# Weight sums of the output projections on VectorE, four low parts moved into the next unit, additions of the plain tiles put first

## The chip, the cores and the metric

The kernel runs on one core of one Trainium2 chip. The metric is the device time of one execution in microseconds (us); the times of a kernel are given as the median of its runs with the lowest and the highest. The core has five engines, each with an instruction queue of its own: TensorE (PE in the profile, its weight loads PEld), VectorE (DVE), ScalarE (ACT), GpSimd (POOL) and SyncE (SP), which here issues the transfers.

## The reference, cut to what matters

Two layers are run over 1024 prompt tokens and 8 sample tokens together. Layer 0 mixes tokens with a gated linear recurrence, layer 1 with a chunked spatial gate. What concerns us is the end of both mixers: an output projection from 2048 to 1024 channels, whose result is added to the residual.

```python
def hgrn2_mixer(h, s0, w_in, lb, g_norm, w_out):
    ...
    return (o * jax.nn.silu(z)) @ w_out, S          # (1032, 2048) @ (2048, 1024)

def chunk_mlp_mixer(h, w_in, ln_g, ln_b, w_sp, b_sp, w_out):
    ...
    y = (u * s * jax.nn.silu(z)) @ w_out             # (1032, 2048) @ (2048, 1024)

def trunk(...):
    ...
        h = h + y
        gate = jax.nn.sigmoid(rmsnorm(h, norm_ple[i]) @ w_ple_gate[i])
        h = h + gate * (p[i] @ w_ple_proj[i])
```

All of it is float32.

## The kernel before, in words

**Products.** Activations lie with channels on the 128 partitions and tokens along the rows. The 1032 tokens are three column blocks, c = 0, 1, 2, of 384, 384 and 264 columns (`CH`, `W`). TensorE is fed with a 32-bit format of its own, so every float32 operand is split into a high part, a cast on ScalarE, and a low part, the difference, on VectorE (`split_weights`, L150 and L151; `split`, L219 and L220; `load_list`, L372 and L376). `mm3` (L224 to L226) makes one product of three matmuls: high times high, high times low, low times high.

**Output projection.** `out_phase` runs once for each layer (keys "oa" and "ob"). The 2048 input channels are taken in two halves of 1024 (f = 0 and 1), the 1024 output channels in eight tiles m of 128. In each half the tiles m = 0 and 1 are "plain": one accumulation in a PSUM bank for each c (`plain`). The tiles 2 to 7 (in the second half 2 to 5) go in pairs through `unit`: seven products instead of eight for the blocks c = 0 and 1, as in a Strassen-Winograd step, and a plain product for c = 2 (`last`). A unit needs four sums of blocks of its weights (s1 to s4) and four sums of blocks of the operand (t1 to t4). Tiles 6 and 7 of the second half are plain again.

**Weights.** `load_unit` fetches two weight tiles of 512 KB with SyncE (L189), forms the four sums in the tile `ssum` with four operations of 512 columns (L193, L195, L198, L200), and splits both tiles and the four sums. Tile names: `wstg` and `wstg3` are staged weights, `whi` and `wlo` the parts of a weight tile, `shi` and `slo` those of a sum. Before the change the four operations run on GpSimd for all units of the kernel. The units of the projection into layer 1 (key "B") pass no f; those of the output projections pass f.

**Additions.** A finished product is added to the residual rows `h` on VectorE (`add`, L1061), directly from PSUM for plain tiles, for c = 2 and for the first of a unit's four results. The three PSUM banks of the tag "mm" (`ps_o`, `ps_proj`) are used in turn by the plain tiles and by the products of a unit: a product can start only when the addition that empties its bank has run. In the second half each addition is followed by a square on ScalarE (`sql`, L259) and its sum on VectorE (`ssq`, L260).

**Inside a unit.** The order of the products on TensorE is: a11 (bank `ps1`), s2, a12 (added onto `ps1`), the c = 2 product of the first tile, s1, s3 (bank `ps_d`), s4, a22 (added onto `ps_d`), the c = 2 product of the second tile. With `early` a c = 2 product comes first. Between a11 and a12 ScalarE copies `ps1` into `u2` (L954), and between s3 and a22 VectorE reads `ps_d` (`c22`, L977). `after(i)` calls hooks between the products.

**Operand of the second half.** While the first half is computed, `mix_second` loads blocks of the second half's operand, forms their sums (`mix_rows`, L418 to L421) and stores them; one step of it (`mix1`) is called from hooks. The last unit of the first half calls `exchange`, which lists 40 transfers for the second half's operand; each step of the list (`jobs`) casts one staged tile, subtracts for its low part (L372, L376) and fetches the tile seven places further on. Twenty steps run in hooks of that unit, twenty behind the first five of the six plain products that follow. The last four of the list belong to t4, which the a22 product of the next unit reads.

**Order.** TensorE's order is the program's. On the other engines a scheduler orders instructions when the program is built; `tc.high_priority(offset=PRI)` moves what it encloses ahead, and `issue_after` holds an instruction behind another. Each engine runs its queue in the order that results. In the profile the output projection of layer 0 lies between about 764 and 935 us, that of layer 1 between about 1614 and 1786 us.

Of the kernel before, what the change touches and what calls it, by code (L numbers as in the profile page):

```python
# [13 lines left out]
ALU = mybir.AluOpType  # L14
# [5 lines left out]
KT = D // P  # L20
# [10 lines left out]
PRI = 400  # L31
# [50 lines left out]
def trunk_kernel(ctx, tc, xT, st, pT, nrm, wina, lbl, gna, wouta, winb, lng, lnb, lngr, lnbr,  # L82
# [95 lines left out]
    def load_unit(key, m, f=None):  # L178


        a = []
        for _ in range(2):

            a.append(ws[0].tile([P, 1024], F32, name="wstg3", bufs=1) if nst[0] % 3 == 2 else
                     wp.tile([P, 1024], F32, name="wstg"))
            nst[0] += 1
        with tc.high_priority(offset=0 if f is None else PRI):
            for i in range(2):
                nc.sync.dma_start(a[i], winb[m + i] if f is None else wsrc[key.lower()][m + i, f])  # L189
        a11, a12, a21, a22 = (a[i][:, j * 512:(j + 1) * 512] for i in range(2) for j in range(2))  # L190
        w0 = split_weights(a[0], 1024, PLAIN, wp)
        t = ws[0].tile([P, 512], F32, name="ssum", bufs=2)
        G.tensor_tensor(t, a21, a22, ALU.add)  # L193
        s1 = split_weights(t, 512, SUMS, ws[0])
        G.tensor_tensor(t, t, a11, ALU.subtract)  # L195
        s2 = split_weights(t, 512, SUMS, ws[0])
        t3 = ws[0].tile([P, 512], F32, name="ssum", bufs=2)
        G.tensor_tensor(t3, a11, a21, ALU.subtract)  # L198
        s3 = split_weights(t3, 512, SUMS, ws[0])
        G.tensor_tensor(t, a12, t, ALU.subtract)  # L200
        s4 = split_weights(t, 512, SUMS, ws[0])
        w1 = split_weights(a[1], 1024, PLAIN, wp)
        return w0, w1, (s1, s2, s3, s4)
# [797 lines left out]
    def out_phase(key, b, ssq, first, done, pre, begin):  # L1001
# [3 lines left out]
        with ExitStack() as s:  # L1005
# [51 lines left out]
            seen = set()  # L1057

            def add(m, c, src, end):
                with tc.high_priority(offset=PRI if end and m >= KT - 2 else 0):  # L1060
                    V.tensor_tensor(hr[c][m], hr[c][m], src[:, :W[c]], ALU.add)  # L1061
                if end:
                    accum_sq(sp, ssq[c], hr[c][m], c not in seen, m == KT - 1, W[c], V if m < 9 else G, True)
                    seen.add(c)
                    if m == KT - 1:
                        done(c)
# [43 lines left out]
            def units(f, ms, then):  # L1110
                for m in ms:
                    wt = take(key.capitalize(), m, f)
                    ex, hooks = then.get(m, (None, {}))
                    bb = dict(b)
                    if ex:
                        ex()
                    unit(wt, bb, up, lambda i, c, src: add(m + i, c, src, f == 1),
                         early=int(f == 0 and m in (2, KT - 2)),
                         then=hooks)
# [29 lines left out]
            def last_exchange():  # L1149
# [1 line left out]
                gen[0] = load_list(quarter("b12"), zr, ZR, False)  # L1151
                steps(gen[0], ZR)()

            units(0, range(2, KT, 2), {2: (rows_of(2), {5: mix1}), 4: (rows_of(4), {1: mix1, 5: mix1, 7: mix1}),
                                       KT - 2: (exchange, {2: jobs(4), 3: jobs(4), 5: jobs(6), 7: jobs(6)})})
            for m in range(2):
                wt = take(key, m, 1)
                for c in CH:
                    ps = plain(bank(), wt, c)
                    if (m, c) != (1, 2):  # L1160
                        jobs(4)()
                    add(m, c, ps, True)
            assert next(gen[0], None) is None
            units(1, range(2, KT - 2, 2), {KT - 4: (last_exchange, {4: jobs(4)})})
            wts = [take(key, m, 1) for m in (KT - 2, KT - 1)]
            for c in CH:
                for m, wt in zip((KT - 2, KT - 1), wts):
# [468 lines left out]
```

## Time and profile before

| what | before |
|---|---|
| median of 3 runs (lowest to highest) | 1910.68 us (1909.73 to 1911.68) |
| profiled execution, its own time | 1912.36 us |
| its span, first to last instruction | 1910.6 us |
| mean granted TensorE clock | 0.988 |

The stages of the two output projections, from a table of stretches of that execution (busy us of each engine; clock as a share of full speed; DMA as mean busy share of the 16 transfer engines):

| stage | stretch | us | PE | DVE | ACT | POOL | clock | DMA |
|---|---|---|---|---|---|---|---|---|
| layer 0, plain tiles, first half | 764 to 792 | 28 | 28.00 | 17.12 | 11.95 | 5.91 | 1.00 | 0.79 |
| layer 0, three units | 792 to 854 | 62 | 60.29 | 46.98 | 20.98 | 11.06 | 1.00 | 0.81 |
| layer 0, plain tiles, second half | 854 to 880 | 26 | 22.66 | 22.51 | 17.77 | 6.05 | 0.98 | 0.67 |
| layer 0, two units and tiles 6, 7 | 880 to 935 | 55 | 55.00 | 34.13 | 18.46 | 5.97 | 0.95 | 0.29 |
| layer 1, plain tiles, first half | 1614 to 1640 | 26 | 25.38 | 15.06 | 14.60 | 4.70 | 1.00 | 0.91 |
| layer 1, three units | 1640 to 1704 | 64 | 59.97 | 44.49 | 19.83 | 11.69 | 1.00 | 0.76 |
| layer 1, plain tiles, second half | 1704 to 1731 | 27 | 24.40 | 24.16 | 17.70 | 6.07 | 1.00 | 0.70 |
| layer 1, two units and tiles 6, 7 | 1731 to 1786 | 55 | 54.09 | 34.49 | 18.62 | 6.38 | 0.94 | 0.24 |

The rest of the profile is read in the prediction. In its rows an arrow `<-` after idle time names what ended the wait; x behind a row counts instructions merged into it.

### The profile page before, as it was taken

What the parts mean: (1) busy time and instruction counts of PE and PEld (TensorE: products, weight loads), DVE (VectorE), ACT (ScalarE), POOL (GpSimd) and SP (SyncE); (2) the same over time, 40 slices, a digit from 0 to 9 for tenths busy, and PEclk for the clock granted to TensorE, in tenths of its full rate; (3) what the DMA queues carried; (4) which work ended last, traced back from release to release, by engine and by line L of the source; (5) the groups of instructions that cost most, each with busy time, mean ns of one, the idle gap of its engine ahead of it and who ended that gap; (6) DMA issues with size and microseconds to landing.
All of it is one profiled execution on the core that took longest, in us unless ns stands there. A gap on an engine that the chain in (4) does not pass through costs nothing.

```text
span 1910.6 us, 34453 instructions
## 1 busy us (share of the span) xinstructions
PE 1869.5 (98%) x13130; PEld 1840.8 (96%) x13130; DVE 1329.5 (70%) x2941; ACT 864.4 (45%) x1853; POOL 448.8 (23%) x445
## 2 busy tenths in 40 slices
PE   8999999999999999999999999999999999999997
PEld 8999999999999999999999999999999999999997
DVE  5967676767767677677664845577778876677655
ACT  6453545444444546434344544433443345344342
POOL 3110001010010001212132323245444551302221
PEclk8999999999999999999999999999999999999998
DMA  6132323333222325873333343323334536872223
GB/s 214 64 116 79 108 72 111 128 127 111 81 91 79 108 67 179 287 232 121 100 120 120 117 143 92 100 81 105 125 126 144 175 104 209 269 236 79 71 89 111
DMA packets 155479, 243.15 MB, mean 127 GB/s; under 512 B 15089, under 2 KB 130481, under 8 KB 154289
## 3 DMA queue, kind: packets, MB, share of 16 engines
q1 hardware_dynamic: 155312, 240.94, 38.5%
q8 instruction: 103, 1.69, 0.4%
q14 instruction: 64, 0.52, 0.1%
HBM read 175.49 MB, written 65.40 MB: 126 GB/s over the span
## 4 chain that ended last, share of the span: by engine, by line
PE 42%; DVE 6%; DMA 4%; issue 2%; ACT 1%; POOL 1%; SPq 0%; DVEq 0%; POOLq 0%; ACTq 0%
PE ps_proj L224 10%; PE ps_proj L226 10%; PE ps_proj L225 10%; PE ps_d L224 2%; PE ps_d L225 2%; PE ps_d L226 2%; DMA raw<-ozd 1%; PE psp L1427 1%; PE pt_g L1309 1%; PE ps_o L224 1%; PE ps_o L225 1%; PE ps_o L226 1%; DMA h<-d3t 1%; DVE bl L376 1%; DVE tmp L298 1%
## 5 line engine op out<-in xcount | busy, mean ns | idle before, releaser
L224 PE MATMUL ps_proj<-bh,whi 128*128 128x384 f32 (+1 forms) x2392 | 766.6, 320 | 9.8 <-DVE h L1061 6.1
L226 PE MATMUL ps_proj<-bh,wlo 128*128 128x384 f32 (+1 forms) x2392 | 750.9, 314 | 1.5 <-DVE wlo L151 1.5
L225 PE MATMUL ps_proj<-bl,whi 128*128 128x384 f32 (+1 forms) x2392 | 749.5, 313 | 1.5 <-POOL bl L220 1.5
L224 PEld LDWEIGHTS ps_proj<-bh,whi 128*128 128x128 f32 x2392 | 452.3, 189 | 12.2 <-issue 6.8
L225 PEld LDWEIGHTS ps_proj<-bl,whi 128*128 128x128 f32 x2392 | 452.6, 189 | 2.0 <-POOL bl L220 2.0
L226 PEld LDWEIGHTS ps_proj<-bh,wlo 128*128 128x128 f32 x2392 | 451.2, 189 | 2.7 <-DVE wlo L151 2.7
L151 DVE TENSOR_TENSOR wlo<-wstg,whi 128x1024 fp32r<-128x1024 f32 x148 | 184.8, 1249 | 100.6 <-ACT whi L150 99.6
L150 ACT CAST whi<-wstg 128x1024 fp32r<-128x1024 f32 x148 | 155.0, 1047 | 139.3 <-PE ps_proj L225 123.0
L150 ACT CAST shi<-ssum 128x512 fp32r<-128x512 f32 x128 | 79.2, 621 | 159.7 <-PE ps_proj L225 77.8
L151 DVE TENSOR_TENSOR slo<-ssum,shi 128x512 fp32r<-128x512 f32 x128 | 102.2, 800 | 15.9 <-ACT shi L150 15.5
L193 POOL TENSOR_TENSOR ssum<-wstg 128x512 f32<-128x512 f32 x32 | 48.4, 1513 | 225.6 <-DMA wstg<-in_winb 69.1
L224 PE MATMUL ps_proj<-xmh,shi 128*128 128x384 f32 x244 | 84.3, 345 | 1.1 <-DVE h L1061 0.8
L225 PE MATMUL ps_proj<-xml,shi 128*128 128x384 f32 x244 | 82.9, 340 | 1.4 <-DVE xml L220 1.4
L226 PE MATMUL ps_proj<-xmh,slo 128*128 128x384 f32 x244 | 82.8, 339 | 0.0
L220 POOL TENSOR_TENSOR ql<-q,qh 128x384 fp32r<-128x384 f32 (+1 forms) x24 | 22.2, 927 | 253.4 <-ACT qh L219 253.4
L716 DVE TENSOR_TENSOR q<-q,t 128x192 f32<-128x192 f32 (+1 forms) x144 | 47.2, 329 | 40.0 <-PE pC L713 33.6
L224 PE MATMUL ps_o<-bh,whi 128*128 128x384 f32 (+1 forms) x232 | 73.2, 315 | 0.0
L225 PE MATMUL ps_o<-bl,whi 128*128 128x384 f32 (+1 forms) x232 | 72.7, 313 | 0.0
L226 PE MATMUL ps_o<-bh,wlo 128*128 128x384 f32 (+1 forms) x232 | 72.6, 313 | 0.0
L1436 POOL TENSOR_TENSOR s<-s,u 128x384 f32<-128x384 f32 (+1 forms) x48 | 54.1, 1128 | 67.7 <-DVE s L1430 67.1
L233 POOL TENSOR_TENSOR rsq<-ss_e,mhalf 128x3 f32<-128x3 f32 (+2 forms) x32 | 24.1, 752 | 194.4 <-DVE ss_e L753 194.4
L195 POOL TENSOR_TENSOR ssum<-ssum,wstg 128x512 f32<-128x512 f32 x32 | 43.2, 1349 | 105.7 <-DVE slo L151 102.7
(339 smaller groups left out, 3958.2 us busy)
## 6 DMA issues: line engine op xcount, KB each, us to landing
wstg<-in_wina SPq DMA_DIRECT2D x48, 512.0 KB, 3.7
wstg<-in_winb SPq DMA_DIRECT2D x48, 512.0 KB, 3.7
raw<-ozd SPq DMA_DIRECT2D x48, 192.0 KB, 3.7
pj<-ppd SPq DMA_DIRECT2D x16, 516.0 KB, 5.0
S<-in_st SPq DMA_DIRECT2D x16, 512.0 KB, 4.5
vb<-vd SPq DMA_DIRECT2D x16, 512.0 KB, 4.8
out_so_s<-S SPq DMA_DIRECT2D x16, 512.0 KB, 3.5
wstg<-in_wouta SPq DMA_DIRECT2D x16, 512.0 KB, 3.9
```

Of the source, the lines that this page charges most:

```text
L150: A.copy(hi, src)
L151: V.tensor_tensor(lo, src, hi.bitcast(F32), ALU.subtract)
L193: G.tensor_tensor(t, a21, a22, ALU.add)
L195: G.tensor_tensor(t, t, a11, ALU.subtract)
L220: last["lo"] = eng.tensor_tensor(lo, src, hi.bitcast(F32), ALU.subtract)
L224: PE.matmul(ps, wh, xh, start=first, stop=False, skip_group_check=more)
L225: PE.matmul(ps, wh, xl, start=False, stop=False, skip_group_check=more)
L226: PE.matmul(ps, wl, xh, start=False, stop=last, skip_group_check=more)
L233: G.tensor_tensor(y, e, mhalf[:, :n], ALU.pow)
L298: V.scalar_tensor_tensor(t[:, :w], src(j), g32[:, gi, j:j + 1], pbc[:, :w], ALU.mult, ALU.mult)
L716: V.tensor_tensor(ql[:, :, 1, :], ql[:, :, 1, :], t2[:, :, 0:1].broadcast_to([P, n, lv]), ALU.mult)
L1436: G.tensor_tensor(s[:, :w], s[:, :w], us[mm, c][:, :w], ALU.mult)
```

## The change

It has three parts. The four weight sums of the units of the output projections (`load_unit` with an f) go from GpSimd to VectorE: five units for each layer, 40 operations in all; the units of the projection into layer 1 keep theirs on GpSimd. Of the twenty steps of the operand exchange behind the plain tiles of the second half the last four move to a hook behind the first product of the next unit. And the additions of the plain tiles m = 0 and 1 of the second half get the high priority that those of tiles 6 and 7 had. Besides, one `mix1` of the second unit of the first half is called one product later.

```diff
--- before.py
+++ after.py
@@ -190,14 +190,15 @@
         t = ws[0].tile([P, 512], F32, name="ssum", bufs=2)
-        G.tensor_tensor(t, a21, a22, ALU.add)
+        eng = G if f is None else V
+        eng.tensor_tensor(t, a21, a22, ALU.add)
         s1 = split_weights(t, 512, SUMS, ws[0])
-        G.tensor_tensor(t, t, a11, ALU.subtract)
+        eng.tensor_tensor(t, t, a11, ALU.subtract)
         s2 = split_weights(t, 512, SUMS, ws[0])
         t3 = ws[0].tile([P, 512], F32, name="ssum", bufs=2)
-        G.tensor_tensor(t3, a11, a21, ALU.subtract)
+        eng.tensor_tensor(t3, a11, a21, ALU.subtract)
         s3 = split_weights(t3, 512, SUMS, ws[0])
-        G.tensor_tensor(t, a12, t, ALU.subtract)
+        eng.tensor_tensor(t, a12, t, ALU.subtract)
@@ -1057,7 +1058,7 @@
             def add(m, c, src, end):
-                with tc.high_priority(offset=PRI if end and m >= KT - 2 else 0):
+                with tc.high_priority(offset=PRI if end and (m >= KT - 2 or m < 2) else 0):
                     V.tensor_tensor(hr[c][m], hr[c][m], src[:, :W[c]], ALU.add)
@@ -1151,17 +1152,16 @@
-            units(0, range(2, KT, 2), {2: (rows_of(2), {5: mix1}), 4: (rows_of(4), {1: mix1, 5: mix1, 7: mix1}),
+            units(0, range(2, KT, 2), {2: (rows_of(2), {5: mix1}), 4: (rows_of(4), {2: mix1, 5: mix1, 7: mix1}),
                                        KT - 2: (exchange, {2: jobs(4), 3: jobs(4), 5: jobs(6), 7: jobs(6)})})
             for m in range(2):
                 wt = take(key, m, 1)
                 for c in CH:
                     ps = plain(bank(), wt, c)
-                    if (m, c) != (1, 2):
+                    if (m, c) < (1, 1):
                         jobs(4)()
                     add(m, c, ps, True)
-            assert next(gen[0], None) is None
-            units(1, range(2, KT - 2, 2), {KT - 4: (last_exchange, {4: jobs(4)})})
+            units(1, range(2, KT - 2, 2), {2: (None, {1: jobs(5)}), KT - 4: (last_exchange, {4: jobs(4)})})
```

TensorE's order is the same in both kernels. In the changed file a line stands one lower between L193 and L1162, so the sums are L194, L196, L199 and L201 there, low parts of the exchange L377, additions to `h` L1062, sums of squares L261 and the read of `ps_d` L978.

VectorE, layer 0, second half, from the addition of tile 0 with c = 2 on (`h_0_10252`; `h_1_10237`, `h_1_10245` and `h_1_10253` are tile 1 with c = 0, 1, 2; `xml` and `bl` are low parts of the exchange), before:

```order
L1061 TENSOR_TENSOR h_0_10252<-h_0_10252,ps_o 128x264
L151 TENSOR_TENSOR wlo<-wstg,whi 128x1024
L376 TENSOR_TENSOR bl_140<-raw,bh_137 128x384
L151 TENSOR_TENSOR slo<-ssum,shi 128x512 x2
L376 TENSOR_TENSOR bl_140<-raw,bh_137 128x384 x3
L151 TENSOR_TENSOR slo<-ssum,shi 128x512
L376 TENSOR_TENSOR bl_140<-zr,bh_137 128x384
L1061 TENSOR_TENSOR h_1_10237<-h_1_10237,ps_o 128x384
L376 TENSOR_TENSOR bl_139<-zr,bh_136 128x384 x2
L260 TENSOR_TENSOR ssq_10263<-ssq_10263,sql 128x384
L376 TENSOR_TENSOR bl_139<-raw,bh_136 128x384 x2
L1061 TENSOR_TENSOR h_1_10245<-h_1_10245,ps_o 128x384
```

The same queue in the changed kernel, in two pieces; first from the two sums of the next unit's weights, which now stand in it, to the addition of tile 1 with c = 0:

```order
L194 TENSOR_TENSOR ssum<-wstg 128x512
L199 TENSOR_TENSOR ssum<-wstg 128x512
L377 TENSOR_TENSOR xml_10221<-raw,xmh_10220 128x384
L151 TENSOR_TENSOR slo<-ssum,shi 128x512
L377 TENSOR_TENSOR bl_140<-zr,bh_137 128x384
L1062 TENSOR_TENSOR h_0_10252<-h_0_10252,ps_o 128x264
L377 TENSOR_TENSOR bl_140<-zr,bh_137 128x384
L151 TENSOR_TENSOR wlo<-wstg,whi 128x1024
L377 TENSOR_TENSOR bl_140<-zr,bh_137 128x384
L377 TENSOR_TENSOR bl_140<-raw,bh_137 128x384
L196 TENSOR_TENSOR ssum<-ssum,wstg 128x512
L377 TENSOR_TENSOR bl_140<-raw,bh_137 128x384
```

The next row is the addition of tile 1 with c = 0 (L1062, `h_1_10237`), and behind it, up to the addition with c = 2:

```order
L151 TENSOR_TENSOR slo<-ssum,shi 128x512 x2
L201 TENSOR_TENSOR ssum<-wstg,ssum 128x512
L377 TENSOR_TENSOR bl_140<-raw,bh_137 128x384 x2
L151 TENSOR_TENSOR slo<-ssum,shi 128x512
L377 TENSOR_TENSOR bl_140<-zr,bh_137 128x384
L1062 TENSOR_TENSOR h_1_10245<-h_1_10245,ps_o 128x384
L261 TENSOR_TENSOR ssq_10263<-ssq_10263,sql 128x384
L377 TENSOR_TENSOR bl_139<-zr,bh_136 128x384
L194 TENSOR_TENSOR ssum<-wstg 128x512
L261 TENSOR_TENSOR ssq_10264<-ssq_10264,sql 128x384
L199 TENSOR_TENSOR ssum<-wstg_11448,wstg 128x512
L1062 TENSOR_TENSOR h_1_10253<-h_1_10253,ps_o 128x264
```

The addition of tile 1 with c = 0 moved ahead of three low parts of weights and of three of the exchange, that with c = 1 ahead of the four of t4 (`bl_139`), and six of the weights' sums now stand among them, the last two (L194, L199) those of the unit after the next.

VectorE at the start of the output projection of layer 1 (`h_0` are additions of tile 0 in the first half, whose banks the first unit needs), before:

```order
L220 TENSOR_TENSOR xml_10221<-h_6_19309,xmh_10220 128x384
L151 TENSOR_TENSOR slo<-ssum,shi 128x512
L220 TENSOR_TENSOR xml_10219<-raw,xmh_10218 128x384
L151 TENSOR_TENSOR slo<-ssum,shi 128x512
L1061 TENSOR_TENSOR h_0_19295<-h_0_19295,ps_o 128x384
```

And in the changed kernel:

```order
L221 TENSOR_TENSOR xml_10221<-h_6_19309,xmh_10220 128x384
L194 TENSOR_TENSOR ssum<-wstg 128x512
L199 TENSOR_TENSOR ssum<-wstg 128x512
L151 TENSOR_TENSOR slo<-ssum,shi 128x512
L221 TENSOR_TENSOR xml_10219<-raw,xmh_10218 128x384
L196 TENSOR_TENSOR ssum<-ssum,wstg 128x512
L1062 TENSOR_TENSOR h_0_19295<-h_0_19295,ps_o 128x384
```

Three sums came in ahead of the first addition, and the second low part of a sum moved behind it.

VectorE in the second unit of the first half, layer 0, where one `mix1` is called later (`raw` are blocks of the second half's operand; the last row reads `ps_d`), before:

```order
L419 TENSOR_TENSOR raw<-raw 128x384
L420 TENSOR_TENSOR raw<-raw 128x384
L1061 TENSOR_TENSOR h_4_10256<-h_4_10256,ps_proj 128x264
L421 TENSOR_TENSOR raw<-raw 128x384
L151 TENSOR_TENSOR wlo<-wstg,whi 128x1024
L970 TENSOR_TENSOR u_10831<-ps_proj,u_10763 128x384
L151 TENSOR_TENSOR slo<-ssum,shi 128x512
L977 TENSOR_TENSOR c_10846<-ps_d,u_10831 128x384
```

And in the changed kernel:

```order
L420 TENSOR_TENSOR raw<-raw 128x384
L1062 TENSOR_TENSOR h_4_10256<-h_4_10256,ps_proj 128x264
L421 TENSOR_TENSOR raw<-raw 128x384
L151 TENSOR_TENSOR wlo<-wstg,whi 128x1024
L971 TENSOR_TENSOR u_10831<-ps_proj,u_10747 128x384
L151 TENSOR_TENSOR slo<-ssum,shi 128x512
L422 TENSOR_TENSOR raw<-raw 128x384
L201 TENSOR_TENSOR ssum<-wstg,ssum 128x512
L978 TENSOR_TENSOR c_10846<-ps_d,u_10831 128x384
```

Between the first of these rows, which waits for a transfer of `raw`, and the read of `ps_d` there is one operation more, a sum.

## The prediction

> **What bounds the kernel now.** I read the page's busy times first, then the list of who TensorE waited for, then, at each wait, the rows of the engines in order of time.
>
> ```profile
> PE 1869.5 (98%) x13130; PEld 1840.8 (96%) x13130; DVE 1329.5 (70%) x2941; ACT 864.4 (45%) x1853; POOL 448.8 (23%) x445
> ...
> PE ps_proj L224 <- DVE h L1061: 6.8, 3, 3.3
> PE ps_d L224 <- DVE c L977: 3.2, 3, 1.6
> ...
> PE ps_proj L224 <- ACT xmh L219: 1.7, 1, 1.7
> ...
> PE ps_proj L225 <- DVE xml L220: 1.4, 1, 1.4
> ```
>
> TensorE is busy 98% of the span, so only its waits, and the slow clock behind them, can be won (columns: total us, times, longest). These four entries, 13.1 us, all lie in the two output projections, which the change touches. The largest stands where the second half's plain tiles end and the next unit begins. TensorE's rows there (start, duration), layer 0, then layer 1:
>
> ```profile
> 876.32 0.28 PE L226 MATMUL ps_o<-bh,wlo 128*128 128x264 f32 x1
> 879.95 0.66 PE L224 MATMUL ps_proj<-bh,whi 128*128 128x384 f32 x1 [3.34 <-DVE h L1061]
> 880.40 0.52 PE L225 MATMUL ps_proj<-bl,whi 128*128 128x384 f32 x1
> ...
> 885.89 0.37 PE L224 MATMUL ps_proj<-xmh,shi 128*128 128x384 f32 x1
> 886.10 0.34 PE L225 MATMUL ps_proj<-xml,shi 128*128 128x384 f32 x1
> 886.27 0.34 PE L226 MATMUL ps_proj<-xmh,slo 128*128 128x384 f32 x1
> ...
> 1728.11 0.28 PE L226 MATMUL ps_o<-bh,wlo 128*128 128x264 f32 x1
> 1731.11 0.41 PE L224 MATMUL ps_proj<-bh,whi 128*128 128x384 f32 x1 [2.71 <-DVE h L1061]
> ...
> 1739.29 0.34 PE L225 MATMUL ps_proj<-bl,whi 128*128 128x384 f32 x1
> ```
>
> At full clock starts lie 0.17 us apart (886.10 to 886.27). After the wait they lie 0.32 apart until 885.89: the clock was halved. From 876.32 to 886.10 there are 9.8 us and 20 steps, one of 264 columns (0.12) and 19 of 0.173, worth 3.4: **6.4 us are lost**. In layer 1, 1728.11 to 1739.29 is 11.2 us for 0.12 and 25 steps, 4.45: **6.7 us lost**. What VectorE did meanwhile:
>
> ```profile
> 870.04 2.58 DVE L376 TENSOR_TENSOR bl<-zr,bh 128x384 fp32r<-128x384 f32 x3
> ...
> 872.89 1.22 DVE L151 TENSOR_TENSOR wlo<-wstg,whi 128x1024 fp32r<-128x1024 f32 x1
> 874.02 0.55 DVE L376 TENSOR_TENSOR bl<-raw,bh 128x384 fp32r<-128x384 f32 x1
> 874.49 1.28 DVE L151 TENSOR_TENSOR slo<-ssum,shi 128x512 fp32r<-128x512 f32 x2
> 875.70 2.57 DVE L376 TENSOR_TENSOR bl<-raw,bh 128x384 fp32r<-128x384 f32 x3
> ...
> 879.26 0.54 DVE L1061 TENSOR_TENSOR h<-h,ps_o 128x384 f32<-128x384 f32 x1
> ```
>
> VectorE has no gap here (the rows left out fill 878.2 to 879.3). The addition that frees the bank (879.26) stands behind low parts nobody needs yet, though its product was done about 870. Before it lies a matter of order, not of work.
>
> **The change, part by part.** *Sums.* 40 operations leave GpSimd for VectorE.
>
> ```profile
> L151 DVE TENSOR_TENSOR slo<-ssum,shi x128: 672/691/1781, 777.6 to 1751.5; 128x512 fp32r<-128x512 f32 x128
> L193 POOL TENSOR_TENSOR ssum<-wstg x32: 1281/1294/2322, 775.7 to 1731.7; 128x512 f32<-128x512 f32 x32
> ...
> 848.32 1.49 DVE L376 TENSOR_TENSOR xml<-raw,xmh 128x384 fp32r<-128x384 f32 x3
> ```
>
> No such sum runs on VectorE before. The nearest row is `slo`: same size, two float32 inputs from SBUF; 0.69 alone, 0.60 a step in a row (1.28 for two). I take 0.60; GpSimd's 1.29 is the upper bound, 0.47 (a step of 384 columns, from 1.49 for three) the lower. What VectorE gets back is seen in the same rows: three low parts take 1.49 at 848.32, but 2.58 at 870.04, while GpSimd adds (its L195 ran at 870.20). About 1.1 us for each clash goes, against 0.6 for the sum, so VectorE's load hardly changes.
>
> *Additions first.* In the order rows the addition for the first bank (tile 1, c = 0) has six low parts fewer ahead of it and three sums more. From which time the new queue runs is set by the weights' transfer, since sums now wait in VectorE's own queue:
>
> ```profile
> 860.96 0.33 SPq L189 DMA_DIRECT2D wstg<-in_wouta  x1
> ...
> 866.72 1.29 POOL L193 TENSOR_TENSOR ssum<-wstg 128x512 f32<-128x512 f32 x1 [37.80 <-DMA wstg<-in_wouta]
> ...
> 885.33 0.42 ACT L259 ACTIVATE sql<-h 128x264 f32<-128x264 f32 x1
> 885.66 0.46 ACT L954 COPY u<-ps_proj 128x384 f32<-128x384 f32 x1
> ...
> 1717.87 1.29 POOL L193 TENSOR_TENSOR ssum<-wstg 128x512 f32<-128x512 f32 x1 [38.57 <-DMA wstg<-in_woutb]
> ...
> wstg<-in_wouta SPq DMA_DIRECT2D x16, 512.0 KB, 3.9
> ```
>
> From 866.7 I add the new rows: up to tile 1's c = 0 addition stand three sums (1.8), six steps of 384 columns (2.8), one `slo` (0.6), one step of 264 (0.34) and one `wlo` (1.13, from 872.89 to 874.02): 6.7 us, so it runs at 873.4. Its bank is due at 876.4: this wait goes. Up to the c = 1 addition come four more steps of 384, three `slo` and a sum, 4.3 us: 877.7, done 878.2, its bank due 12 matmuls behind the first, at 878.5. Up to the c = 2 addition come four steps and two sums, 3.1 us: 880.8; its bank is due at 882.7. But on ScalarE its square stands ahead of the copy `u2` (885.33, 885.66), without which a12 cannot begin: 0.42 for the addition, 0.35 for the square and 0.46 for the copy give 882.0, while a12 is due at 876.44 + 24 x 0.173 = 880.6. So a **new wait of 1.4 us** appears, up to 2.1 where VectorE also waits for a high part or for the next weights; I take 1.9. In layer 1 the weights land at 1717.87 and a12 is due at 1732.4: 0.8 to 1.5, I take 1.3. Gains: 6.4 - 1.9 = 4.5 and 6.7 - 1.3 = 5.4.
>
> *Four low parts moved.* Four casts, four subtractions (1.9 us of VectorE) go behind the c = 1 addition; no transfer goes with them, as the list's fetches run seven steps ahead. They are read by a22, 14 us later: cost nothing; within the sum above.
>
> *Heads of the first units.*
>
> ```profile
> 787.61 0.33 SPq L189 DMA_DIRECT2D wstg<-in_wouta  x1
> 787.98 3.29 SPq L1221 DMA_DIRECT2D h<-d0t  x7
> ...
> 798.59 0.45 PE L225 MATMUL ps_proj<-xml,shi 128*128 128x384 f32 x1 [1.40 <-DVE xml L220]
> ...
> 1637.52 1.54 POOL L195 TENSOR_TENSOR ssum<-ssum,wstg 128x512 f32<-128x512 f32 x1 [0.63 <-DVE slo L151]
> ...
> 1640.35 1.35 DVE L1061 TENSOR_TENSOR h<-h,ps_o 128x384 f32<-128x384 f32 x3
> ...
> 1641.05 0.36 PE L224 MATMUL ps_proj<-bh,whi 128*128 128x264 f32 x1 [1.66 <-ACT xmh L219]
> ```
>
> In layer 1 the bank's addition (1640.35) waits behind a `slo` for GpSimd's L195; with sums of 0.6 it ends near 1638.2, before its due time 1639.2: -1.7, less 0.2 where the next sum waits for its weights. In layer 0 seven row fetches (787.98), the last of which the waited-for `xml` reads, stand in SyncE's queue behind a weight fetch that a missing buffer holds until 787.61. Now three of the seven stand ahead of it (1.4 us of issue at 0.47 each), and the buffer comes free earlier, by four sums 0.7 shorter less two operations put ahead, about 1.8 us. Together 3.2 us against a wait of 1.4: -1.4.
>
> *Second units.*
>
> ```profile
> 1673.78 0.56 DVE L419 TENSOR_TENSOR raw<-raw 128x384 f32<-128x384 f32 x1 [3.93 <-DMA raw<-ozd]
> ...
> 1677.85 0.55 DVE L977 TENSOR_TENSOR c<-ps_d,u 128x384 f32<-128x384 f32 x1
> ```
>
> L419 waits for a transfer and `c` follows 4.1 us behind it; now L200 stands between: +0.6 in layer 1, where TensorE waits for `c`, +0.2 in layer 0, where it waited 0.2. The late `mix1` moves no transfer ahead; the stores and fetches of `raw` keep to the same releases within 1 us. I count 0 for the third wait (1.6, third units).
>
> **Sum**: -4.5 - 5.4 - 1.5 - 1.4 + 0.8 = -12.0 us. The profiled execution took 1912.36 us (1.8 around its span), 1.7 above the median; it would become 1900.4, and the median 1910.7 - 12.0 = **1898.7**.
>
> **Rivals.**
>
> *The clock halves again.* Which wait is long enough?
>
> ```profile
> 753.28 0.69 PE L759 MATMUL pt_o<-ident,on 128*128 128x128 f32 x2 [2.37 <-DVE ss_e L753]
> ...
> 754.09 0.52 PE L225 MATMUL ps_pple<-bl,whi 128*128 128x384 f32 x1
> 754.41 0.52 PE L226 MATMUL ps_pple<-bh,wlo 128*128 128x384 f32 x1
> ```
>
> 2.37 us was enough (steps of 0.32 after it), 1.66 at 1641.05 was not. My new waits of 1.9 and 1.3 lie near that. The price is what the first case shows, 18 steps at 0.32 for 0.17, 2.8 us each: 1901.5 with one, 1904.3 with both. [...]
>
> *The DMA sets the pace.* TensorE comes earlier to transfers that do not: the heads' 2.9 us are waited out later (third units), the new waits grow by 0.6 each and halve the clock: -12.0 + 2.9 + 1.2 + 5.6 = -2.3, so 1908.4. For it: L419's 3.93 idle. Against it: the stores that gate these fetches follow VectorE, which follows TensorE.
>
> *Slower: weights late in VectorE's queue.* GpSimd could wait 37.80 us for weights and hurt nobody; VectorE's sums hold up everything behind them, the banks' additions too. The transfer took 5.8 us (860.96 to 866.72). If it lands x later, the new waits are 1.9 + x and 1.3 + x, with halved clock 2.8 each: 1898.7 + 5.6 + 2x. Slower by 0.2% needs x above 5.1; at 6 it is 1916.3. For it: transfers are dense there; against: such a fetch lands after 3.9 us in the median. [...]
>
> That the change does not do what it says is excluded by the order rows.
>
> **How the numbers follow.** Forecast 0.62, clock 0.20, DMA pace 0.11, slower 0.07. If all new waits and the third units' 1.6 vanished, 1898.7 - 3.2 - 1.6 = 1893.9: the low end, 1894. The high end, 1907, takes both halved clocks (1904.3) and 1.3 more on each new wait. A sum at GpSimd's 1.29 adds 0.69 x 6 = 4.1 to each new wait, with the clock 1912.5; at 0.47, 0.8 less each; the first is left outside. This kernel's measurement tells 0.2%, 3.8 us, from no change: faster 0.82, same 0.11, slower 0.07.
>
> **What would show it.** Right: TensorE's 6.8 us for h L1061 falls below 1; a12 waits 1 to 2 us for the copy `u2` in both layers; no steps of 0.32 near 880 and 1732; no waits at 798 and 1641; sums of 0.6 to 0.7 on VectorE. Wrong: sums idle for weights while TensorE waits for `h`; waits for `c` grown past 2 us; half clock in the second half.

## The result, and the profile after

| | before | after |
|---|---|---|
| median of 5 runs (lowest to highest) | 1911.66 us (1909.73 to 1916.78) | 1900.86 us (1895.89 to 1902.93) |
| profiled execution, its own time | 1912.36 us | 1900.86 us |
| its span | 1910.6 us | 1899.1 us |
| mean granted TensorE clock | 0.988 | 0.992 |

The ratio of the times is 0.9937, with a 95% interval of 0.9916 to 0.9957 (the two medians alone lie 10.8 us apart); the forecast was a gain of 12.0 us, 0.9937. A second measurement of the same kernel, shown below, gave 0.9950 (0.9934 to 0.9966).

First the changed kernel's page (its first table: busy us, share of the span, instructions), then its list of waits over the whole span (total us, times, longest):

```profile
PE 1864.6 (98%) x13130; PEld 1835.7 (97%) x13130; DVE 1337.9 (70%) x2981; ACT 864.3 (46%) x1853; POOL 391.2 (21%) x405
```

```profile
PE ps_d L225 <- DVE c L978: 3.8, 5, 2.3
...
PE ps_proj L225 <- ACT u L955: 2.0, 2, 1.4
```

GpSimd lost 57.6 us of busy time, VectorE gained only 8.4 with forty operations more. The waits for `h`, `xml` and `xmh` (6.8, 1.4 and 1.7 us before) are no longer in the list. The copy `u2` (L955) is in it, as the prediction had it.

TensorE's order is the same in both kernels, so each matmul of before has its counterpart, and the difference of their starts tells where time is won. The gain of each stage, from such pairs at its two ends, us (minus is faster):

| stage | forecast | first profile | second profile |
|---|---|---|---|
| all up to the first output projection | 0 | +0.6 | -0.2 |
| layer 0, head of the first unit | -1.4 | -1.6 | -1.6 |
| layer 0, first half's units | +0.2 | -0.3 | +0.6 |
| layer 0, plain/unit boundary | -4.5 | -4.7 | -4.2 |
| between the two projections | 0 | +1.9 | +1.6 |
| layer 1, head of the first unit | -1.5 | -1.9 | -1.9 |
| layer 1, second unit | +0.6 | -1.2 | -0.2 |
| layer 1, third unit | 0 | +2.3 | -0.2 |
| layer 1, plain/unit boundary | -5.4 | -6.7 | -4.4 |
| from there to the end | 0 | 0 | 0 |
| sum | -12.0 | -11.6 | -10.5 |

At the boundary of layer 0, the changed kernel's rows in order of time (start, duration): TensorE (the matmul that had waited 3.34 us, then the first of a12), VectorE (the first sum, and the additions with c = 0, 1, 2 of tile 1) and ScalarE:

```profile
875.13 0.34 PE L225 MATMUL ps_proj<-bh,whi 128*128 128x384 f32 x1
...
880.83 0.44 PE L225 MATMUL ps_proj<-xmh,whi 128*128 128x384 f32 x1 [1.37 <-ACT u L955]
```

```profile
864.99 0.69 DVE L194 TENSOR_TENSOR ssum<-wstg 128x512 f32<-128x512 f32 x1 [1.08 <-DMA wstg<-in_wouta]
...
871.69 0.55 DVE L1062 TENSOR_TENSOR h<-h,ps_o 128x384 f32<-128x384 f32 x1
...
875.96 0.55 DVE L1062 TENSOR_TENSOR h<-h,ps_o 128x384 f32<-128x384 f32 x1
...
879.47 0.42 DVE L1062 TENSOR_TENSOR h<-h,ps_o 128x264 f32<-128x264 f32 x1
```

```profile
879.99 0.42 ACT L260 ACTIVATE sql<-h 128x264 f32<-128x264 f32 x1 [1.44 <-DVE h L1062]
880.32 0.46 ACT L955 COPY u<-ps_proj 128x384 f32<-128x384 f32 x1
```

The three additions come 6.7, 11.0 and 14.5 us behind the first sum; the prediction's queue had them at 6.7, 11.0 and 14.1. The last is 0.4 later, nearly all of it because a sum waited 0.34 for its weights. Then the square, then the copy, and a12 waits 1.37 us (forecast 1.4 to 2.1, 1.9 taken). No half clock follows: the next steps lie 0.17 apart (881.12, 881.29). The one half clock in the two projections is at the third unit of layer 1:

```profile
1697.10 0.61 PE L225 MATMUL ps_d<-xmh,whi 128*128 128x384 f32 x1 [2.33 <-DVE c L978]
1697.51 0.52 PE L226 MATMUL ps_d<-xml,whi 128*128 128x384 f32 x1
1697.83 0.52 PE L227 MATMUL ps_d<-xmh,wlo 128*128 128x384 f32 x1
...
1700.68 0.34 PE L227 MATMUL ps_d<-xmh,wlo 128*128 128x384 f32 x1
```

Behind the wait of 2.33 us ten steps lie 0.32 apart instead of 0.17, 1.5 us more.

### The profile page after: what moved, and what is told of

It reads as the page before. It is cut to its first block, busy times and chain, and to the rows that moved or that the text cites. A ratio compares the mean times of both kernels' runs of the same rounds, so it can differ in the third digit from the quotient of the medians.

```text
span 1899.1 us, 34403 instructions
## 1 busy us (share of the span) xinstructions
PE 1864.6 (98%) x13130; PEld 1835.7 (97%) x13130; DVE 1337.9 (70%) x2981; ACT 864.3 (46%) x1853; POOL 391.2 (21%) x405
## 4 chain that ended last, share of the span: by engine, by line
PE 82%; DVE 8%; DMA 6%; ACT 2%; issue 1%; POOL 1%; SPq 0%; DVEq 0%; ACTq 0%; POOLq 0%
PE ps_proj L225 19%; PE ps_proj L227 19%; PE ps_proj L226 19%; PE ps_d L225 2%; PE ps_d L227 2%; PE ps_d L226 2%; PE ps_o L225 2%; PE ps_o L226 2%; PE ps_o L227 2%; DMA raw<-ozd 2%; PE psp L1427 1%; PE pC L714 1%; PE pt_o L760 1%; DMA d1t<-raw 1%; PE p L680 1%
## 5 line engine op out<-in xcount | busy, mean ns | idle before, releaser
L234 POOL TENSOR_TENSOR rsq<-rms_e,mhalf 128x3 f32<-128x3 f32 x15 | 14.1, 940 | 379.5 <-DVE rms_e L278 379.5
L1177 DVE TENSOR_TENSOR tmp<-tmp,pj 128x384 f32<-128x384 f32 (+1 forms) x48 | 25.2, 525 | 56.1 <-ACT tmp L1176 50.1
```

The source lines that it names most:

```text
L234: G.tensor_tensor(y, e, mhalf[:, :n], ALU.pow)
L1177: V.tensor_tensor(gt[:, :w], gt[:, :w], pj[:, OFF[c]:OFF[c] + w], ALU.mult)
```

## The experiments

The two theories of the first four runs differ on why the boundary was late. Theory O is the prediction's own sentence: before it lies a matter of order, not of work, so the priority and the moved low parts win the time. Theory G: GpSimd's sums make VectorE's queue late, by their length and by stretching VectorE's steps, and the order hardly matters.

**Sums alone** (`e1_sums_only`), the kernel before with

```diff
-        G.tensor_tensor(t, a21, a22, ALU.add)
+        eng = G if f is None else V
+        eng.tensor_tensor(t, a21, a22, ALU.add)
```

and the same for the other three sums.

> The kernel before with the forty weight sums on VectorE and nothing else changed (additions not put first, no low part moved, no mix1 moved). Theory O (order; the prediction's words, a matter of order and not of work): the two heads' waits go (1.4 + 1.7 us), but at the two boundaries the addition of tile 1, c = 0 still stands behind all low parts, TensorE's waits for h L1062 stay near 3 us each with half clock behind them: about 3 us faster than before, 1908.5. Theory G (GpSimd: the sums' own 1.29 us and the clashes with VectorE's low parts set how late the queue is): adding 0.47, 0.6 and 1.13 us a step from the changed kernel's own first sum (864.99) gives that addition at 875.3, against a due time of 875.1, and the next at 878.1 against 877.9: two waits of 0.7 us, no half clock, so about 10 us faster than before, 1901.5.

1899.58 us against 1911.29, ratio 0.9939 (0.9922 to 0.9956): the whole gain of the changed kernel, with no priority and no step moved. VectorE at the boundary of layer 0:

```profile
866.94 0.69 DVE L194 TENSOR_TENSOR ssum<-wstg 128x512 f32<-128x512 f32 x1 [0.36 <-DMA wstg<-in_wouta]
...
868.65 0.69 DVE L151 TENSOR_TENSOR slo<-ssum,shi 128x512 fp32r<-128x512 f32 x1
869.26 1.49 DVE L377 TENSOR_TENSOR bl<-zr,bh 128x384 fp32r<-128x384 f32 x3
870.66 0.42 DVE L1062 TENSOR_TENSOR h<-h,ps_o 128x264 f32<-128x264 f32 x1
...
877.49 0.55 DVE L1062 TENSOR_TENSOR h<-h,ps_o 128x384 f32<-128x384 f32 x1
```

and the rows of the kernel before that answer to them and to the stretch between, beside those in the prediction:

```profile
867.64 0.78 DVE L376 TENSOR_TENSOR xml<-raw,xmh 128x384 fp32r<-128x384 f32 x1 [2.05 <-ACT xmh L372]
868.69 1.43 DVE L151 TENSOR_TENSOR slo<-ssum,shi 128x512 fp32r<-128x512 f32 x1 [0.27 <-ACT shi L150]
...
872.55 0.42 DVE L1061 TENSOR_TENSOR h<-h,ps_o 128x264 f32<-128x264 f32 x1
...
878.19 0.68 DVE L151 TENSOR_TENSOR slo<-ssum,shi 128x512 fp32r<-128x512 f32 x1
```

From the first sum to the addition of tile 1 with c = 0 it is 10.55 us (866.94 to 877.49); in the kernel before it was 12.54 (866.72 to 879.26), though four sums (2.4 us) less stood in VectorE's queue. So 4.4 us went elsewhere. Three steps took longer, start to start: the `slo` at 868.69 1.35 instead of 0.60, the three low parts at 870.04 2.51 and those at 875.70 2.49 instead of 1.40 each; together 2.95. The rest, 1.5, lies at the front, in the 1.97 us ahead of the first `slo`, where VectorE had one low part to do: it waited 0.92 us for that low part's operand, took 0.31 longer over it, and waited 0.27 for the high part of GpSimd's first sum. With the sums on VectorE the first two of them, 1.2 us, fill that time. TensorE's waits for `h` there are 0.96 and 0.48 instead of 3.34 us, and the half clock behind them is gone, 3.1 of the 6.4 us that were lost.

**Additions first alone** (`e2_first_only`), the kernel before with

```diff
-                with tc.high_priority(offset=PRI if end and m >= KT - 2 else 0):
+                with tc.high_priority(offset=PRI if end and (m >= KT - 2 or m < 2) else 0):
```

> The kernel before with the additions of the plain tiles 0 and 1 of the second half put first, and nothing else. Theory O: the waits at the two boundaries go, about 9 us faster, 1902.5, with the heads' waits (1.4 and 1.7 us) left. Theory G: the addition of tile 1, c = 0 comes in time (875.7 in the trace of before, due 876.6), but the steps it has overtaken (3.6 us there), a sum of squares and two low parts now stand before the addition with c = 1: 881.5 against 878.7, so the wait of about 3 us moves one product on and the clock halves as before: within 1.5 us of before, 1910 to 1912.

1910.32 against 1911.29, ratio 0.9994 (0.9980 to 1.0007): nothing. Its VectorE, the additions with c = 0 and c = 1 of layer 0, and TensorE's row:

```profile
872.70 0.54 DVE L1061 TENSOR_TENSOR h<-h,ps_o 128x384 f32<-128x384 f32 x1
...
878.04 0.55 DVE L1061 TENSOR_TENSOR h<-h,ps_o 128x384 f32<-128x384 f32 x1
```

```profile
878.73 0.41 PE L224 MATMUL ps_proj<-xmh,shi 128*128 128x384 f32 x1 [2.38 <-DVE h L1061]
```

The addition that was put first is in time; the next one is 2.4 us late, and the clock halves as before (steps of 0.32 us from 879.71 on). The wait moved on by one product, as theory G had it.

**Sums back on GpSimd** (`e3_no_sums`), the changed kernel with `eng = G`.

> The changed kernel with the weight sums back on GpSimd: additions first, the four low parts and the mix1 moved. Theory O: 3 us slower than the changed kernel (the heads' waits come back), 1904. Theory G: as the kernel with the additions first alone, since VectorE's order at the boundaries is the same: 9 us or more slower than the changed kernel, 1910, with waits of 2.5 to 3.5 us for h at c = 1 and half clock in both layers.

1912.94 against 1911.29, ratio 1.0016 (1.0002 to 1.0030): the three other parts together win nothing. Waits of 0.8 (layer 0) and 2.6 us (layer 1) for `h` are followed by 2.5 and 1.9 us for the copy `u2`, and half clock follows in layer 0 alone. So theory G had the time right, but in layer 0 most of the wait moved on to the copy instead of staying at `h`, and the half clock that it gave for layer 1 did not come.

**Without the priority** (`e4_no_first`), the changed kernel with `m >= KT - 2` in `add` as before.

> The changed kernel without the priority for the additions of the plain tiles 0 and 1. Theory O: most of the gain at the boundaries goes, waits of 2 us or more for h come back, 6 us or more slower than the changed kernel, 1907 or more. Theory G: the addition of tile 1, c = 0 moves behind four more steps and two sums, from 871.7 to 875.5, due 875.1: one wait of about 0.9 us in each layer, within 2 us of the changed kernel, 1901 to 1903.

1898.69 against 1911.29, ratio 0.9934 (0.9917 to 0.9952). Waits for `h` are 1.0 us in layer 0 and 1.9 in layer 1, where theory G gave 0.9 for each; the one in layer 1 has half clock behind it (see the last section). In return no a12 waits for the copy.

**GpSimd made busy again** (`e5_collide`), the kernel with the sums alone and

```diff
+        if f == 1 and "a" in key.lower():
+            g = ws[0].tile([P, 184], F32, name="gsum", bufs=1)
+            for x, y in ((a21, a22), (a11, a21), (a21, a11), (a12, a11)):
+                for o in (0, 164, 328):
+                    G.tensor_tensor(g, x[:, o:o + 184], y[:, o:o + 184], ALU.add)
         return w0, w1, (s1, s2, s3, s4)
```

> The kernel with the sums alone on VectorE, and in the second half of layer 0 twelve more additions for each unit on GpSimd (128x184, read the unit's weights, into a tile that nobody reads). VectorE's and SyncE's order stay as in the kernel with the sums alone. It parts theory G in two. G-length (only GpSimd's longer sums, 1.29 against 0.69 us, delayed VectorE's queue): nothing waits for the new additions, so the time stays, 1899.6, and from the first sum to the addition of tile 1, c = 0 it stays 10.6 us (866.94 to 877.49). G-clash (VectorE's own steps take longer while GpSimd adds: 2.58 and 2.57 us for three low parts against 1.49, in the trace of before): some 3 us of stretch come back, that stretch is 13 us or more, TensorE waits 3 us or more for h L1062 in layer 0, with half clock behind it: 5 us slower than the sums alone, 1904.5.

1904.32 against 1910.02, ratio 0.9976 (0.9965 to 0.9986): 4.7 us behind the sums alone by the medians, 7 by the ratios, where 5 were expected. GpSimd's twelve additions in layer 0, VectorE beside them, and TensorE's wait:

```profile
862.21 11.52 POOL L208 TENSOR_TENSOR gsum<-wstg 128x184 f32<-128x184 f32 x12 [105.55 <-DMA wstg<-in_wouta]
```

```profile
862.10 0.69 DVE L194 TENSOR_TENSOR ssum<-wstg 128x512 f32<-128x512 f32 x1 [0.44 <-DMA wstg<-in_wouta]
862.71 1.08 DVE L199 TENSOR_TENSOR ssum<-wstg 128x512 f32<-128x512 f32 x1
...
865.55 2.65 DVE L382 TENSOR_TENSOR bl<-zr,bh 128x384 fp32r<-128x384 f32 x3
868.13 0.42 DVE L1067 TENSOR_TENSOR h<-h,ps_o 128x264 f32<-128x264 f32 x1
...
875.87 0.54 DVE L382 TENSOR_TENSOR bl<-zr,bh 128x384 fp32r<-128x384 f32 x1
...
876.95 0.54 DVE L1067 TENSOR_TENSOR h<-h,ps_o 128x384 f32<-128x384 f32 x1
```

```profile
877.63 0.66 PE L230 MATMUL ps_proj<-bh,whi 128*128 128x384 f32 x1 [5.23 <-DVE h L1067]
```

Nobody reads what GpSimd adds here. While it adds, three low parts take 2.65 us instead of 1.49, and a sum 1.08 instead of 0.69; behind it (875.87) a low part takes 0.54. The addition to `h`, one of whose inputs comes from PSUM, takes its usual 0.42 in the midst of it. From the first sum to the addition it is 14.85 us instead of 10.55. So the clash by itself, without any wait for GpSimd, makes VectorE's queue 4.3 us late. Not every operation beside GpSimd is slowed: the low part of a whole tile (`wlo`, 128x1024), between the rows shown, took 1.26 us instead of 1.22. Why the one is stretched and the other not isn't shown, as no run varied where the inputs lie. Here GpSimd was busy for 11.5 us; in the kernel before, its four sums took some 6. By pairs of matmuls the boundary of layer 0 costs 6.1 us more than in the kernel with the sums alone. That of layer 1, where GpSimd adds nothing, costs 1.7 us more too (one wait of 2.5 us for `h` with half clock behind it, in place of 1.6 and 0.5); this part can't be put down to the clash.

**The square behind the copy** (`e6_copy_first`), the changed kernel with

```diff
-                if end:
+                if end and (m, c) == (1, 2):
+                    held.append((m, c))
+                elif end:
+                    square(m, c)
+
+            held = []
+
+            def square(m, c):
+                with tc.issue_after(rest["u2"].ins) if held else ExitStack():
                     accum_sq(sp, ssq[c], hr[c][m], c not in seen, m == KT - 1, W[c], V if m < 9 else G, True)
...
-            units(1, range(2, KT - 2, 2), {2: (None, {1: jobs(5)}), KT - 4: (last_exchange, {4: jobs(4)})})
+            units(1, range(2, KT - 2, 2), {2: (None, {1: jobs(5), 2: lambda: (square(*held[0]), held.pop())}), KT - 4: (last_exchange, {4: jobs(4)})})
```

> The changed kernel with one thing moved: the square of tile 1, c = 2 stands behind the copy u2 on ScalarE instead of ahead of it. If the prediction's new wait (a12 waits for the copy behind the square, 1.37 us in layer 0, none in layer 1) is as it says, the copy no longer waits for the addition at 879.47, but for the cast whi that ends about 878.5; it is done at 879.0, a12 is due at 879.46: the wait goes, 1.4 us in layer 0 and 0 in layer 1, 1899.5. If the copy waits for something else (the bank, a11), the wait stays, 1900.9.

1894.72 against 1910.02, ratio 0.9918 (0.9905 to 0.9932). No a12 waits for the copy in either layer. ScalarE in layer 0:

```profile
873.91 1.04 ACT L150 CAST whi<-wstg 128x1024 fp32r<-128x1024 f32 x1
874.85 0.47 ACT L955 COPY u<-ps_proj 128x384 f32<-128x384 f32 x1
876.42 0.42 ACT L260 ACTIVATE sql<-h 128x264 f32<-128x264 f32 x1 [1.09 <-DVE h L1062]
```

The copy stands right behind the cast, and the square waits for the addition alone. The gain was larger than the 1.4 us expected; the second profiles of both kernels, below, take that up.

**Low parts not moved** (`e7_no_move`), the changed kernel with `if (m, c) != (1, 2)` and no `jobs(5)`, as before.

> The changed kernel with the four low parts back behind the plain tiles, additions still first. If the move matters, a wait for h of 2 us or more comes back and it is 3 us or more slower, 1904. If the sums on VectorE are all that matters, the addition with c = 2 comes at 878.8 against 879.5 (four low parts instead of two sums and one low part), nothing new waits, and it is within 1 us of the changed kernel: 1900 to 1901, with the wait for the copy 0.7 instead of 1.4 us in layer 0.

1897.37 against 1910.02, ratio 0.9937 (0.9924 to 0.9949), the changed kernel's own ratio. The wait for the copy is 0.69 us in layer 0, as expected, and 1.53 in layer 1.

**Both** (`e8_combined`), the square behind the copy and the low parts not moved.

> Sums on VectorE, additions first, the four low parts not moved, the mix1 moved, the square behind the copy u2. By the sums of the two runs before, no wait over 0.4 us is left at either boundary: 1.4 us faster than the changed kernel, 1899.5. The waits for c in the second and third units have been 0 to 2.4 us in the profiles so far, with no order to it, so the total can miss that by 2 us either way. If the four low parts ahead of the addition with c = 2 make it late, a wait for h or for the copy of 1 to 2 us shows instead, 1901 to 1902.

1896.07 against 1910.02, ratio 0.9927 (0.9914 to 0.9941). At the boundaries one wait of 0.55 us for `h` in layer 1 is left. It can't be told from the square behind the copy alone.

**The changed kernel again** (`e9_after_again`), no edit.

> The changed kernel once more, for a second profile and a comparison on one chip with the next. At the first boundary the same rows, so the same wait for the copy u2 in layer 0 (1.2 to 1.5 us) and none in layer 1. Theory D (the waits for c in the third units follow the transfers of the exchange and differ from execution to execution): they differ from the first profile's (0.2 us in layer 0, 2.3 us in layer 1) by more than 0.5 us in one of the two. Theory R (they belong to this kernel's order of instructions): the same within 0.3 us. On the clock, theory W (it is judged in stretches of 3.413 us on a fixed grid; so far all 18 stretches with 1.80 us or more of TensorE idle had half clock behind them, all 10 with 1.3 to 1.70 us had not): every half clock's end lies a multiple of 3.413 us from the others. Rival: the length of one wait decides, 1.8 us or more. 1900.9 again, by the first comparison's interval 1896 to 1903.

1900.58 against 1910.82, ratio 0.9950 (0.9934 to 0.9966). TensorE's waits in this profile, in the output projection of layer 0, then of layer 1:

```profile
PE ps_proj L225 <- ACT u L955: 1.7, 1, 1.7
PE ps_d L225 <- DVE c L978: 1.1, 1, 1.1
```

```profile
PE ps_d L225 <- DVE c L978: 2.6, 2, 1.4
PE ps_proj L225 <- ACT u L955: 1.7, 1, 1.7
```

The waits for `c` are others than in the first profile (layer 0: 1.1 for 0.2; layer 1: 1.2 and 1.4 for 0.2 and 2.3), so theory R is out: they differ from execution to execution. That they follow the transfers, the other half of theory D, agrees with the rows: ahead of layer 1's third unit ScalarE waited 4.18 us for a transfer of `raw` in the first profile and 3.65 in this one, and the low parts of what it then cast stand ahead of `c` in VectorE's queue. No run varied the transfers alone. And the copy's wait in layer 1, forecast 1.3 by the prediction, absent in the first profile and so not expected for this run, is 1.7 here. The reason lies in VectorE's first sum there, in the first profile and in this one:

```profile
1710.97 0.69 DVE L194 TENSOR_TENSOR ssum<-wstg 128x512 f32<-128x512 f32 x1
```

```profile
1712.73 0.69 DVE L194 TENSOR_TENSOR ssum<-wstg 128x512 f32<-128x512 f32 x1 [1.37 <-DMA wstg<-in_woutb]
```

In the first profile TensorE began the unit 12.3 us behind that sum (1723.30), in this one, where the sum waited for its weights, 9.4 us (1722.13); in layer 0 of the first it was 10.1. So the copy is late when the first sum comes too shortly ahead of the unit, as the prediction had it. In the five places where this order of instructions had the wait (both profiles, and the kernel with the mix1 back, below), the lead and the wait add up to 11.1 to 11.9 us. A late transfer of weights is one cause of a short lead, but not the only one: in layer 0 of this profile the first sum waited for no transfer, came 9.4 us ahead, and a12 waited 1.65. On the clock, no wait of this profile's projections has half clock behind it, the longest stretch of idle time in the grid being 1.73 us.

**The square behind the copy again** (`e10_copy_again`).

> The changed kernel with the square of tile 1, c = 2 behind the copy u2, once more beside the changed kernel on one chip. If only the wait for the copy went, it is 1.4 us faster than the changed kernel; the first comparison gave 1894.7 against 1900.9, 6 us, on different chips. Two terms could make more of it than 1.4: the third units' waits (by chance, then it shrinks to 1 to 2 us here) or something that the moved square sets free later in layer 0 or 1 (then 4 us or more again).

1896.97 against 1910.82, ratio 0.9929 (0.9912 to 0.9945), 3.6 us faster than the changed kernel on the same chip. No wait for the copy in either layer. The expectation of 1.4 us had counted the first profile's single wait; the second profile has two, 1.65 and 1.73, together 3.4, and neither is in this profile. The waits for `c` differ too (1.3 in layer 0 and 0.8 in layer 1 here, 1.1 and 2.6 there), so how much of the measured 3.6 us belongs to the square is told only by those rows. No version that ran is faster; the one with the low parts not moved either (0.9927) can't be told from it.

**First halves' sums alone on VectorE** (`e11_f1_gpsimd`), the changed kernel with `eng = V if f == 0 else G`.

> The changed kernel with the sums of the second halves' units back on GpSimd, those of the first halves left on VectorE. The prediction's terms for the heads (1.5 and 1.4 us) and nothing at the boundaries: about 3 us faster than before, 0.9985, with waits of 2 us or more for h or the copy u2 at both boundaries and no waits at the heads. If the heads' terms do not hold by themselves, it is the same as before; if the boundaries need no VectorE sums of their own second half, it is as fast as the changed kernel.

1905.75 against 1910.82, ratio 0.9977 (0.9963 to 0.9991): 4.4 us, where the heads' terms gave 2.9. The heads have no wait; at the boundaries TensorE waits 3.0 and 2.9 us for `h` at c = 1, with half clock behind (in layer 1 steps of 0.32 us from 1725.73 on).

**The mix1 back** (`e12_mix_back`), the changed kernel with `{1: mix1, 5: mix1, 7: mix1}`.

> The changed kernel with the one mix1 called where it was before. The prediction counted nothing for it: within 1.5 us of the changed kernel, no wait for c over 0.5 us in the second units (those of before, 0.2 and 1.4 us, went with GpSimd's sums). If the later mix1 is what took the second unit's wait away in layer 1, that wait of 1.4 us comes back; if the later mix1 makes the third units' waits, they go and it is 1 to 3 us faster.

1901.86 against 1910.82, ratio 0.9952 (0.9934 to 0.9970), as the changed kernel. No wait for `c` in layer 1's second unit: it was not the later `mix1` that took it away.

All parts beside each other:

| sums on VectorE | additions first | low parts moved | mix1 later | ratio to before (95%) |
|---|---|---|---|---|
| no | yes | no | no | 0.9994 (0.9980 to 1.0007) |
| no | yes | yes | yes | 1.0016 (1.0002 to 1.0030) |
| yes | no | no | no | 0.9939 (0.9922 to 0.9956) |
| yes | no | yes | yes | 0.9934 (0.9917 to 0.9952) |
| yes | yes | no | yes | 0.9937 (0.9924 to 0.9949) |
| yes | yes | yes | no | 0.9952 (0.9934 to 0.9970) |
| yes | yes | yes | yes | 0.9937 (0.9916 to 0.9957), 0.9950 (0.9934 to 0.9966) |

## Why the prediction was right, and where not

- **The sum and its large terms held.** -12.0 us (0.9937) was forecast; the two measurements gave 0.9937 and 0.9950, the two profiles -11.6 and -10.5 us. The two boundaries gave -4.7 and -6.7 (second profile -4.2 and -4.4) for -4.5 and -5.4, the two heads -1.6 and -1.9 for -1.4 and -1.5. The mechanism of layer 0's head is in SyncE's rows: the weight fetch that a buffer holds went out at 786.63 us (787.61 before) with three more of the row fetches ahead of it, and the last of them was issued by 788.86 instead of 791.27.
- **That the total came within 0.4 us is partly luck.** In the first profile 1.9 us lost between the projections and 2.3 in layer 1's third unit, for which the sum has nothing, were made up by 1.8 us more than forecast in layer 1's second unit and 1.3 at its boundary.
- **The queue was worked out right**, to 0.0, 0.0 and 0.4 us for the three additions, because its steps were taken at their length without GpSimd beside them. A sum on VectorE takes 0.69 alone and 0.60 in a row (864.99 to 865.60 in the changed kernel), as taken from `slo`.
- **The reading "a matter of order, not of work" was wrong.** That sentence and the heading "additions first" gave the gain to the priority. Alone the priority wins nothing, with the other parts but without the sums it doesn't either, and without it the changed kernel is as fast. The clashes that the prediction set off against the sums ("VectorE's load hardly changes") were the matter: VectorE's 2.4 us more of sums took the place of 2.95 us of stretch and of 1.5 us at the front, most of it idle.
- **The new wait for the copy `u2`** came as forecast, by the same two rows on ScalarE: 1.37 and none in the first profile, 1.65 and 1.73 in the second, for 1.9 and 1.3. Together that is 1.4 and 3.4 us for 3.2. Moving the one square removed them; a wait of 0.2 to 0.4 us for `c` in layer 1's unit behind the boundary appeared with it in both of its profiles.
- **The second and third units were mis-sized.** +0.6 for a sum ahead of `c` in layer 1 measured -1.2 and -0.2, and 0 for the third unit +2.3 and -0.2. The two profiles of the same kernel differ by more than the term; by the prediction's own rival these waits follow the transfers. In the first profile this cost 2.3 us, of which 1.5 is half clock behind a wait of 2.33: a wait for `c` past 2 us was one of the prediction's own signs of being wrong, and it showed there.
- **Between the projections** 1.6 to 1.9 us were lost, which no term has. The largest of these losses stand at TensorE's waits for `c` and for the copy `u2` in the projection into layer 1, which the change leaves alone. Kernels with all sums on GpSimd lose 0.3 and 0.9 us there too, the others 0.4 to 2.1, all against the one profile of before. That this is more than the luck of that execution isn't shown.
- **The rival of late weights** shows its mechanism in small: the sum that waited 1.37 us for its weights in the second profile's layer 1 goes with a wait of 1.73 us for the copy. It stayed far from the 5.1 us from which it would have decided.
- **The clock** halved behind none of the new waits (1.37, 1.65, 1.73), as forecast; but the threshold read from two rows (2.37 us is enough, 1.66 is not) is none, see below.

## What to carry to other kernels

Work moved off a busy VectorE onto GpSimd was not free here even where nobody waited for it: count what VectorE's own steps lose beside it (here three low parts took 2.5 us instead of 1.4) and compare that with the cost of doing the work on VectorE. Try each part of a change alone before the gain is given to one of them; of the four here a single one did it all. And look for what is late next: here a square ahead of a copy in ScalarE's queue made waits of 1.4 to 1.7 us, and the kernel without them was 3.6 us faster, though other waits differed too.

## What the runs showed of the clock

In these runs half clock did not follow from the length of a wait. TensorE's rows of two kernels: without the priority (layer 1), and with the mix1 back (layer 0).

```profile
1720.28 0.41 PE L225 MATMUL ps_proj<-bh,whi 128*128 128x384 f32 x1 [1.89 <-DVE h L1062]
...
1720.98 0.52 PE L225 MATMUL ps_proj<-bh,whi 128*128 128x384 f32 x1
1721.30 0.52 PE L226 MATMUL ps_proj<-bl,whi 128*128 128x384 f32 x1
```

```profile
884.17 0.44 PE L225 MATMUL ps_proj<-xmh,whi 128*128 128x384 f32 x1 [2.15 <-ACT u L955]
...
884.80 0.34 PE L225 MATMUL ps_proj<-xmh,whi 128*128 128x384 f32 x1
884.98 0.33 PE L226 MATMUL ps_proj<-xml,whi 128*128 128x384 f32 x1
```

A wait of 1.89 us was followed by steps of 0.32, one of 2.15 by steps of 0.17. Within one trace the half clock ends on a grid: in the kernel before at 12.14, 22.38, 36.04, 49.70, 885.97 and 1739.30, which lie 506.00, 503.00, 499.00, 495.00 and 250.00 times 3.4133 us before the last. The trace itself gives the step: neighbouring ends lie 10.24, 13.66 and 13.66 us apart, and its granted clock is 0.50 for 3.41 us from 752.83 on and for 6.83 us from 879.12 and from 1732.46 on. With such a grid in each of the fourteen traces, from 700 us to 20 us before the end, all 25 stretches in which TensorE idled 1.80 us or more have half clock in the next stretch, eight of them also in the one after; none of the 20 with 1.31 to 1.74 us has. Ten of these 45 are of the last four runs, taken after the theory was on record; the expectation's count of the earlier ones, 18 and 10, is lower than the 20 and 15 found here. The wait of 2.15 us lies across a grid point, with about 0.9 us ahead of it and 1.3 behind. So between the dense matmuls of this stretch a wait of up to about 1.7 us cost only itself, and a longer one 1.5 us more for one stretch, 3 for two, or nothing, by where it fell; the prediction's price of 2.8 us was that of two stretches.

Near both ends of the program, where TensorE also runs matmuls of one column, idle time did not tell it. TensorE's rows in the kernel with the mix1 back:

```profile
16.68 2.73 PE L275 MATMUL pss<-ones,sq 128*128 128x1 f32 x24
...
19.71 0.52 PE L226 MATMUL ps_pple<-pl,whi 128*128 128x384 f32 x1
20.04 0.52 PE L227 MATMUL ps_pple<-ph,wlo 128*128 128x384 f32 x1
```

Behind 24 such matmuls without a gap the steps lie 0.33 apart. In the last 20 us of eight traces a stretch with only 1.54 to 1.59 us of idle time, and one-column matmuls beside it, has half clock behind it. So idle time alone did not decide it there; what the matmuls of one column do to the clock isn't shown, as no run varied them by themselves.

Of the fourteen times that half clock came in the projections TensorE had been idle for a whole stretch only once, in the 5.23 us of the run with GpSimd made busy; in the others a stretch idle for a little over half, 1.80 us or more of 3.41, was enough.
